# A depthwise convolution's sample rows as one GpSimd product and one VectorE sum, and four shifts of each tile moved from TensorE to VectorE

## The chip, the cores and the metric

The kernel runs on one core of one Trainium2 chip. The metric is the time of one execution on the device, in microseconds. A core has five engines that run side by side and wait for one another by semaphores: TensorE (PE in the profile; PEld is its loading of weights), VectorE (DVE), ScalarE (ACT), GpSimd (POOL) and SyncE (SP, which here issues DMAs). Each engine takes its own instructions strictly in the order in which the program issued them, so an instruction that waits holds up all that stand behind it on the same engine.

## The reference

The reference is one inference step of a small decoder trunk of two layers. It is run for a prompt of 256 tokens and for 8 samples of 4 new tokens each; both groups use the same weights. Layer 0 mixes tokens with sparse attention, layer 1 with a Conformer convolution module, and each mixer is followed by a feed-forward part that has a short convolution of its own. The change lies in the Conformer module of layer 1:

```python
def causal_dwconv(x_pad, w, b):
    c = x_pad.shape[-1]
    y = lax.conv_general_dilated(x_pad, w[:, None, :], window_strides=(1,), padding='VALID',
                                 dimension_numbers=('NWC', 'WIO', 'NWC'), feature_group_count=c)
    return y + b

def conformer_conv(x, hist, w_pw1, b_pw1, w_dw, b_dw, ln_g, ln_b, w_pw2, b_pw2):
    a, gate = jnp.split(x @ w_pw1 + b_pw1, 2, axis=-1)
    a = a * jax.nn.sigmoid(gate)
    a_pad = jnp.concatenate([hist, a], axis=1)
    h = jax.nn.silu(layer_norm(causal_dwconv(a_pad, w_dw, b_dw), ln_g, ln_b))
    return h @ w_pw2 + b_pw2, a_pad[:, -(CONV_WIDTH - 1):]
```

The width of the convolution is 31, there are 2048 channels, and every channel has its own 31 weights. For the prompt the 30 rows ahead of the first token are zero. For a sample they are rows of earlier tokens, given as an input; each of its 4 outputs is the sum of 30, 29, 28 or 27 products with given rows and 1, 2, 3 or 4 products with rows that this step computes.

## The kernel before

Activations lie with the channels on the 128 partitions: 16 tiles of 128 channels, each with 288 columns (256 of the prompt, then 8 times 4 of the samples). A matrix product with weights runs as float32 in three products of halves: ScalarE rounds a slab of weights to its high part (`pump`, L180), VectorE subtracts it from the slab for the low part (L182), and TensorE multiplies high by high, high by low and low by high (L259 to L261). The split slabs have three buffers, so the split of a slab runs at most a few slabs ahead of the matmuls that use it.

The order of all instructions is written out by the program, by a planner with lanes. `gemm` issues matmuls and after each piece calls `tick` with the microseconds that the piece is taken to last on PE. Each lane collects these as credit, and as long as it has credit it issues the next step of the generator at its head; a generator says with `yield` how much credit its step costs. Here the lanes are `ev` (what follows a group's matmuls), `bg` (`conv`) and `bg2` (`spread_out`), and `bg2` goes on only where `ev` is empty.

The Conformer module multiplies by `w_pw1` in 14 groups: two groups of two channel tiles each, then twelve groups of one. After a group, `glu` (L1746) writes the gated rows of tile j: those of the prompt into `apad` (L1760), those of the samples into the last four places of each of the 8 rows of `hist` (L1761). `past` holds the samples' sums over the given rows with the bias added; it was computed much earlier (`history`, L1677), by GpSimd products over shifted views (L1699) and VectorE sums (L1681).

The 31 taps of a prompt tile are shared out over three engines:

- ScalarE multiplies by the first `NACT` = 4 taps (L1808, L1811), and GpSimd adds these up (L1812) in the tile `ac`.
- VectorE adds the taps from `NACT` to `4 * PEM - 2`, one instruction of 256 columns each (L1824). With `PEM` = 3 these are the taps 4 to 10, seven of them. The first reads `ac`, the others go on in place in `cy`.
- TensorE takes the last 20 taps in 5 sets of 4 (L1840), each matmul with a 32-column block of a matrix `dg`, whose diagonals GpSimd fills with weights (L1801). Its moving operand `xt` holds shifted copies of the tile. SP writes the tile to DRAM (L1797) and reads it back in four pieces (L1819).

`spread_out(j)` (L1789) issues for a tile, in this order: the copy of its last rows (L1795), the write to DRAM, the `dg` product, the four ScalarE products with their adds, the four sample instructions (`samples`, L1780), the loads of `xt`, and the seven VectorE taps. `conv(j)` (L1828) then takes the mean from the tile on GpSimd (L1836, from tile 4 on), issues the matmuls, adds their result on VectorE (L1844), and lets `shifted` (L326) take the tile into the layer norm's sums (ScalarE square L330, GpSimd sums L335 and L336). Thus on GpSimd the instruction L1836 of one tile, which waits for the tile's last tap, stands ahead of the adds L1812 of the next.

`samples(j, d)` is one VectorE instruction: to the outputs from place d on it adds the new rows times the weight 30 - d. Four of them, for d = 0 to 3, with 32, 24, 16 and 8 elements for each partition, complete the samples' columns of a tile; the first also adds `past`.

Tile 15 has no group behind it that would hide it, and `conv_last` (L1857) computes it after the last group: its shifted copies come from matmuls (L1869) and ScalarE copies (L1871), and VectorE adds the taps 1 to 10 (L1885, L1887) with the sample instructions between them. L1891 joins both, and the layer norm follows. At the start of the stage `ready()` (L1739) issues two memsets and three DMAs on GpSimd, which at that time also adds to the sums of the layer norm before (L335, L336). These are then joined by VectorE (L356, L357) and summed over the partitions by PE (L372, L373).

Of the kernel before, what the change touches and what calls it, by code (L numbers as in the profile page):

```python
# [7 lines left out]
F32 = mybir.dt.float32  # L8
# [6 lines left out]
AF = mybir.ActivationFunctionType  # L15
OP = mybir.AluOpType
AX = mybir.AxisListType

D = 2048
NT = 16  # L20
TP = 256
NS, TS = 8, 4
# [8 lines left out]
CW = 31  # L31
# [16 lines left out]
NDG = 1  # L48
# [3 lines left out]
PRW = (6.0, 14.0, 9.0)  # L52
DOT = 0.35
DOTW = 5.0
PEM, NACT = 3, 4
BIS = (1.8, 0.3)
LST = (2.2, 2.2, 2.2, 1.5, 1.2, 0.9, 5.0)
ROPE = 0.5
# [6 lines left out]
ALAG = 5  # L65
LEADS = 12
SUBP = (1, 3)
CLAG = (3.2, 5.6, 5.0, 1.0)
LW = (1.2, 0.5, 0.8, 2.0, 1.4, 0.8, 16, 1.2, 1.45, 1.2)

QC, KC, VC, QIC, KIC = 0, 2048, 2560, 3072, 4096
# [574 lines left out]
def trunk(ctx, tc, a, o, stages=9):  # L646
    k = K(ctx, tc, a, o)
    nc = k.nc
# [19 lines left out]
    ap = st.enter_context(tc.tile_pool(name="attn", bufs=1))  # L668
# [42 lines left out]
    p = pb()  # L711
# [203 lines left out]
    def sample_index():  # L915
# [150 lines left out]
        for b in range(9):  # L1066
            s_ = 1 << b
            n_ = 512 - s_
            nc.vector.tensor_scalar(m[:, s_:], x_[:, s_:], 1 << (15 + b), None, op0=OP.bitwise_and)
            nc.vector.copy_predicated(x_[:, :n_], m[:, s_:], x_[:, s_:])  # L1070
            k.v(1.2)
            if p is None and (b == 8 or k.now > ready):
                p = total(1)
                nc.tensor.matmul(p[:, 1:2], lower, cnt, start=True, stop=True)
            yield LST[3]
# [598 lines left out]
    hist = hp.tile([128, NT, NS, CW - 1 + TS], F32, name="hist")  # L1674
    past = hp.tile([128, NT, NS * TS], F32, name="past")
# [32 lines left out]
    fp = sf.enter_context(tc.tile_pool(name="ffn0", reuse_waits="tile", bufs=1))  # L1708
# [15 lines left out]
    fp = sf.enter_context(tc.tile_pool(name="conf", reuse_waits="tile", bufs=1))  # L1724
    cy = fp.tile([128, NT, T], F32, name="cy")
# [8 lines left out]
    zero = fp.tile([128, last, CW], F32, name="zero")  # L1734
    tapm = fp.tile([128, 32], F32, name="tapm")
    wdq = fp.tile([128, NT * 32], F32, name="wdq")
    pads = {}

    def ready():  # L1739
        nc.gpsimd.memset(zero, 0.0)  # L1740
        nc.gpsimd.memset(lpad[:, 0:30], 0.0)
        nc.gpsimd.dma_start(tapm, a["consts"][:, CO["tapm"][0]:CO["tapm"][0] + 32])
        nc.gpsimd.dma_start(wdq, a["w_dq"])
        nc.gpsimd.dma_start(spread.rearrange("(j p) u -> p j u", p=128)[:, :, :CW], zero)
# [32 lines left out]
    dlane = Lane()  # L1777
    k.lanes.append(dlane)

    def samples(j, d):  # L1780

        sv = cy[:, j, TP:].rearrange("p (s t) -> p s t", t=TS)[:, :, d:]
        prev = past[:, j].rearrange("p (s t) -> p s t", t=TS) if d == 0 else sv
        nc.vector.scalar_tensor_tensor(sv, hist[:, j, :, CW - 1:CW - 1 + TS - d], k.par("w_dw", j * CW + CW - 1 - d),  # L1784
                                       prev, op0=OP.mult, op1=OP.add)

    spreads = {}

    def spread_out(j):  # L1789

        if j == 0:
            yield 10.0
        pad = pads.pop(j)
        t = pad[:, 30:]
        nc.gpsimd.tensor_copy(tailp[:, j], t[:, TP - CW + 1:])  # L1795
        rows = spread[j * 128:(j + 1) * 128]
        nc.sync.dma_start(rows[:, CW:], t)  # L1797
        nm = 8 - PEM
        dg = fp.tile([128, 4, nm, 32], F32, name="dg", bufs=2)
        wq = wdq[:, 32 * j:32 * j + 32].rearrange("p (i m) -> p i m", m=8)[:, :, PEM:]  # L1800
        nc.gpsimd.tensor_tensor(dg, wq[:, :, :, None].to_broadcast([128, 4, nm, 32]),  # L1801
                                tapm[:, None, None, :].to_broadcast([128, 4, nm, 32]), op=OP.mult)
        tap = lambda q_: (k.par("w_dw", j * CW + q_), pad[:, q_:q_ + TP])
        pl = fp.tile([128, TP], F32, name="ac", bufs=2)
        for q_ in range(NACT):
            w, src = tap(q_)
            if q_ == 0:
                nc.scalar.activation(pl, src, AF.Identity, bias=k.par("b_dw", j), scale=w)  # L1808
            else:
                d_ = fp.tile([128, TP], F32, name="ad", bufs=3)  # L1810
                nc.scalar.activation(d_, src, AF.Copy, scale=w)  # L1811
                nc.gpsimd.tensor_tensor(pl, pl, d_, op=OP.add)  # L1812
            yield CLAG[0] / 8
        for d in range(TS):
            samples(j, d)
            yield CLAG[0] / 8
        xt = fp.tile([128, 4, 284 - 4 * PEM], F32, name="xt", bufs=3)
        for i in range(4):
            nc.sync.dma_start(xt[32 * i:32 * i + 32],  # L1819
                              rows[:, i + 4 * PEM:i + 284].rearrange("(g c) u -> c g u", c=32))  # L1820
        acc = cy[:, j, :TP]
        for q_ in range(NACT, 4 * PEM - 1):
            w, src = tap(q_)
            nc.vector.scalar_tensor_tensor(acc, src, w, pl if q_ == NACT else acc, op0=OP.mult, op1=OP.add)  # L1824
            yield CLAG[1] / 7
        spreads[j] = dg, xt

    def conv(j):  # L1828
# [9 lines left out]
        for m in range(PEM, 8):  # L1838
            for i in range(4):
                nc.tensor.matmul(p[32 * i:32 * i + 32, :TP], dg[:, i, m - PEM],  # L1840
                                 xt[:, i, 4 * (m - PEM):4 * (m - PEM) + TP],
                                 start=m == PEM, stop=m == 7, skip_group_check=True)
        yield CLAG[2]
        nc.vector.tensor_tensor(cy[:, j, :TP], cy[:, j, :TP], p[:, :TP], op=OP.add)  # L1844
        if j < lnc.H:
            yield CLAG[3]
            lnc.first(j)
# [4 lines left out]
        else:  # L1852
            yield CLAG[3]
            lnc.shifted(j)
            yield 0.4

    def conv_last():  # L1857

        j = last
        k.drain(dlane)  # L1860
        lnc.stats(1)
        pc = pp()
        nc.tensor.matmul(pc[:, :T], nident, lnc.c, start=True, stop=False)
        w0 = 4 * LM - 1
        xt = fp.tile([128, 4, TP + 4 * (7 - LM)], F32, name="lxt")
        for g_ in range(4):
            ps_ = pp()
            for i in range(4):
                nc.tensor.matmul(ps_[32 * i:32 * i + 32, :xt.shape[2]], k.ident[:, 32 * g_:32 * g_ + 32],  # L1869
                                 lpad[:, w0 + i:w0 + i + xt.shape[2]], start=True, stop=True, skip_group_check=True)  # L1870
            nc.scalar.activation(xt[:, g_], ps_[:, :xt.shape[2]], AF.Copy)  # L1871
        lnc.stats()
        for q_ in range(1, NDG):
            nc.tensor.matmul(pc[:, :TP], diag[:, q_], lpad[:, q_:q_ + TP], start=False, stop=False)
        for m in range(LM, 8):
            for i in range(4):
                nc.tensor.matmul(pc[32 * i:32 * i + 32, :TP], ldg[:, i, m - LM],
                                 xt[:, i, 4 * (m - LM):4 * (m - LM) + TP],
                                 start=False, stop=False, skip_group_check=True)
        nc.tensor.matmul(pc[:, :TP], diag[:, 0], lpad[:, :TP], start=False, stop=True)  # L1880
        acc = cy[:, j, :TP]
        for q_ in range(NDG, w0):
            w, src = k.par("w_dw", j * CW + q_), lpad[:, q_:q_ + TP]
            if q_ == NDG:
                nc.vector.tensor_scalar(acc, src, w, k.par("b_dw", j), op0=OP.mult, op1=OP.add)  # L1885
            else:
                nc.vector.scalar_tensor_tensor(acc, src, w, acc, op0=OP.mult, op1=OP.add)  # L1887
            if q_ - NDG < TS:
                samples(j, q_ - NDG)
        nc.gpsimd.tensor_copy(tailp[:, j], lpad[:, 256:])  # L1890
        nc.vector.tensor_tensor(cy[:, j], cy[:, j], pc[:, :T], op=OP.add)  # L1891
        lnc.table()
        lnc.lag = 0
        lnc.shifted(j)
        k.pump(g_pw1[-1].first + len(g_pw1[-1].slabs) - 1)

    k.bg.cap, k.bg2.after = CAP, k.ev
    ready()
    dlane.append(diags())
    tailp = fp.tile([128, NT, CW - 1], F32, name="tailp")  # L1900
    for gi, g in enumerate(g_pw1):
# [11 lines left out]
        if js[-1] < last:  # L1913
            for j in js:
                k.bg2.append(spread_out(j))
                k.bg.append(conv(j))
    k.drain(k.bg2, k.bg, k.ev)
    conv_last()
    k.bg.cap, k.bg2.after = 3.0, None
    nc.gpsimd.dma_start(o["conv_p"].rearrange("p (j w) -> p j w", j=NT), tailp)  # L1920
# [99 lines left out]
def build(a):  # L2020
    import concourse.bacc as bacc
    nc = bacc.Bacc("TRN2", target_bir_lowering=False, num_devices=1)
    ins = {n: nc.dram_tensor(n, v.shape, mybir.dt.from_np(v.dtype), kind="ExternalInput").ap() for n, v in a.items()}
    outs = {n: nc.dram_tensor("out_" + n, s, F32, kind="ExternalOutput").ap() for n, s in _OUT.items()}
    with tile.TileContext(nc) as tc:
        with ExitStack() as ctx:
            trunk(ctx, tc, ins, outs)
    return nc
# [25 lines left out]
```

## Time and profile before

| | us |
|---|---|
| timed runs: lowest, median, highest of 3 | 2581.97, 2583.43, 2583.6 |
| the profiled execution, whole | 2581.04 |
| its span, from the first to the last instruction | 2579.2 |
| PE convolution matmuls L1840, first to last start | 1411.8 to 1588.7 |

The profile is one execution, taken by the hardware profiler. Its page gives each engine's busy time over the span, the chain of work that ended last, and the costliest groups of instructions. An engine's busy share over the whole span is an average over stages, so for one stage it is read from a table by windows. Rows of instructions give the start in us from the start of the span, the duration in us, the engine, the line of the program, the operation, what it writes and reads, shapes and count; a bracket at the end gives the engine's idle time just before and what ended it. Several instructions of one kind in a row are merged into one row with their count. On PE the matmuls are pipelined: each shows some 0.3 us, and yet a new one starts every 0.13 us. The page has the engines' share in the chain that ended last:

```profile
PE 88%; DVE 7%; ACT 2%; issue 2%; POOL 1%; DMA 1%; SPq 0%; another core or an unknown queue 0%; ACTq 0%; DVEq 0%; POOLq 0%
```

### The profile page before, as it was taken

To read this page: it belongs to the slowest core of one execution; us is meant where nothing else is said; L and a number is where in the kernel's file an instruction comes from. 1 tells how busy PE (TensorE), PEld (TensorE's weight loads), DVE (VectorE), ACT (ScalarE), POOL (GpSimd) and SP (SyncE) were. 2 spreads that over 40 slices of the span, in tenths; PEclk is the share of its full clock that TensorE was granted. 3 is DMA by queue.
4 is the path that set the end of the run, shared out by engine and by line. 5 is a ranking of instruction groups with operands and counts; after the bars stand their busy time and mean duration, and the time that the engine had idled before them with its cause. 6 is when DMAs were issued, how large, how long until landed. Compare 5 with 4: busy or idle time off the path is not lost.

```text
span 2579.2 us, 48375 instructions
## 1 busy us (share of the span) xinstructions
PE 2529.2 (98%) x19597; PEld 2434.7 (94%) x19597; DVE 1612.4 (63%) x2505; ACT 1172.3 (45%) x1864; POOL 653.6 (25%) x913
## 2 busy tenths in 40 slices
PE   9999899999999999999999999999999999999997
PEld 9789559999999999999999887999999999999997
DVE  5678446686665455555659997778555444555554
ACT  4464344564443334444446444656444333444444
POOL 1153541432221101011236564352010000111123
PEclk9999999999999999999999999999999999999999
DMA  9745865555555555556555655555545555555653
GB/s 349 211 129 193 284 230 185 165 177 188 161 169 167 159 172 162 167 163 162 177 164 171 181 165 182 163 165 164 166 162 172 164 160 168 163 170 163 172 164 103
DMA packets 152512, 454.81 MB, mean 176 GB/s; under 512 B 26224, under 2 KB 46880, under 8 KB 151008
## 3 DMA queue, kind: packets, MB, share of 16 engines
q1 hardware_dynamic: 139744, 400.04, 49.7%
q0 software_dynamic: 12016, 51.09, 5.8%
q8 instruction: 153, 2.51, 0.4%
q14 instruction: 71, 0.58, 0.1%
q10 hardware_dynamic: 528, 0.59, 0.1%
HBM read 438.37 MB, written 13.30 MB: 175 GB/s over the span
## 4 chain that ended last, share of the span: by engine, by line
PE 88%; DVE 7%; ACT 2%; issue 2%; POOL 1%; DMA 1%; SPq 0%; another core or an unknown queue 0%; ACTq 0%; DVEq 0%; POOLq 0%
PE pt L261 25%; PE pt L260 25%; PE pt L259 25%; DVE wl L182 2%; PE pg L259 2%; PE pg L261 2%; PE pg L260 2%; PE tr L1360 1%; DVE cy L1824 1%; PE pt L1840 1%; ACT wh L180 1%; PE m L1422 1%; PE pg L939 1%; PE sc L1381 0%; DVE cy L1784 0%
## 5 line engine op out<-in xcount | busy, mean ns | idle before, releaser
L182 DVE TENSOR_TENSOR wl<-raw,wh 128x1024 fp32r<-128x1024 f32 (+2 forms) x713 | 883.7, 1242 | 749.3 <-ACT wh L180 743.8
L180 ACT ACTIVATE wh<-raw 128x1024 fp32r<-128x1024 f32 (+1 forms) x732 | 761.8, 1044 | 836.4 <-PE pt L260 695.0
L261 PE MATMUL pt<-xh,wl 128*128 128x288 f32 (+1 forms) x3520 | 1040.1, 295 | 3.9 <-DVE wl L182 3.8
L260 PE MATMUL pt<-xl,wh 128*128 128x288 f32 (+1 forms) x3520 | 1041.9, 296 | 0.1
L259 PE MATMUL pt<-xh,wh 128*128 128x288 f32 (+1 forms) x3520 | 1041.0, 296 | 0.9 <-ACT xh L1481 0.9
L261 PEld LDWEIGHTS pt<-xh,wl 128*128 128x128 f32 x3520 | 665.4, 189 | 6.1 <-DVE wl L182 5.9
L259 PEld LDWEIGHTS pt<-xh,wh 128*128 128x128 f32 x3520 | 662.8, 188 | 7.7 <-issue 5.8
L260 PEld LDWEIGHTS pt<-xl,wh 128*128 128x128 f32 x3520 | 663.3, 188 | 0.4 <-DVE xl L1482 0.3
L261 PE MATMUL pt<-hh,wl 128*128 128x288 f32 (+1 forms) x1664 | 495.1, 298 | 0.0
L260 PE MATMUL pt<-hl,wh 128*128 128x288 f32 (+1 forms) x1664 | 493.8, 297 | 0.0
L259 PE MATMUL pt<-hh,wh 128*128 128x288 f32 (+1 forms) x1664 | 492.3, 296 | 0.0
L1597 POOL COPY sto<-gpad 128x2 f32<-128x2 f32 x88 | 85.2, 968 | 970.7 <-ACT gpad L1590 970.5
L260 PEld LDWEIGHTS pt<-hl,wh 128*128 128x128 f32 x1664 | 313.8, 189 | 0.1
L259 PEld LDWEIGHTS pt<-hh,wh 128*128 128x128 f32 x1664 | 313.4, 188 | 0.1
L261 PEld LDWEIGHTS pt<-hh,wl 128*128 128x128 f32 x1664 | 312.7, 188 | 0.0
L259 PE MATMUL pg<-xh,wh 128*128 128x288 f32 (+1 forms) x528 | 164.5, 312 | 0.8 <-ACT wh L180 0.8
L261 PE MATMUL pg<-xh,wl 128*128 128x288 f32 (+1 forms) x528 | 156.9, 297 | 1.8 <-DVE wl L182 1.7
L260 PE MATMUL pg<-xl,wh 128*128 128x288 f32 (+1 forms) x528 | 156.7, 297 | 0.6 <-DVE xl L285 0.4
L1601 ACT ACTIVATE s<-y,pvec 128x304 f32<-128x304 f32 x88 | 48.5, 551 | 161.2 <-DVE y L1596 161.2
L259 PEld LDWEIGHTS pg<-xh,wh 128*128 128x128 f32 (+1 forms) x528 | 99.3, 188 | 9.8 <-issue 7.9
L260 PEld LDWEIGHTS pg<-xl,wh 128*128 128x128 f32 (+1 forms) x528 | 99.2, 188 | 4.1 <-issue 2.6
L261 PEld LDWEIGHTS pg<-xh,wl 128*128 128x128 f32 (+1 forms) x528 | 99.3, 188 | 3.3 <-DVE wl L182 3.2
(370 smaller groups left out, 2289.9 us busy)
## 6 DMA issues: line engine op xcount, KB each, us to landing
raw<-w SPq DMA_DIRECT2D x705, 512.0 KB, 3.5
xt<-spread SPq DMA_DIRECT2D x60, 136.0 KB, 4.3
raw<-w SPq DMA_DIRECT2D x16, 296.0 KB, 6.6
kid<-kvt POOLq DMA_DIRECT2D x4, 1024.0 KB
kvt<-kid SPq DMA_DIRECT2D x8, 512.0 KB, 9.2
x<-xT POOLq DMA_DIRECT2D x1, 2304.0 KB
raw<-w SPq DMA_DIRECT2D x6, 384.0 KB, 3.1
out_y<-x SPq DMA_DIRECT2D x16, 144.0 KB, 1.8
```

Source lines behind the costliest of these rows:

```text
L180: nc.scalar.activation(wh[:, :n], r[:, :n], AF.Copy)
L182: eng.tensor_tensor(wl[:, :n], r[:, :n], wh[:, :n].bitcast(F32), op=OP.subtract)
L259: nc.tensor.matmul(out, wh[:, c:c + w], xh, start=st, stop=False)
L260: nc.tensor.matmul(out, wh[:, c:c + w], xl, start=False, stop=False)
L261: nc.tensor.matmul(out, wl[:, c:c + w], xh, start=False, stop=sp)
L939: nc.tensor.matmul(p[:, :512], qb[:, pr], kx[pr][:, 512 * i:512 * i + 512], start=True, stop=True)
L1360: nc.tensor.transpose(p[:, h * 128:(h + 1) * 128], g[:, h * 128:(h + 1) * 128], ident)
L1422: nc.tensor.matmul(po[32 * h:32 * h + 16, :128], z[:, c, i, h], g[:, 512 + h * 128:640 + h * 128], start=False, stop=(i == TS - 1 and c == ...
L1597: nc.gpsimd.tensor_copy(sto[:, j, 0:2], gp[:, 256:258])
L1601: nc.scalar.activation(s[:, :304], y[:, :304], AF.Silu, bias=k.par(bc, j))
L1824: nc.vector.scalar_tensor_tensor(acc, src, w, pl if q_ == NACT else acc, op0=OP.mult, op1=OP.add)
L1840: nc.tensor.matmul(p[32 * i:32 * i + 32, :TP], dg[:, i, m - PEM], xt[:, i, 4 * (m - PEM):4 * (m - PEM) + TP], start=m == PEM, stop=m == 7, ...
```

## The change

The samples' new rows are no longer four VectorE instructions. At the start of the stage GpSimd builds `wnew`, which has for each channel and each of the 4 output places a row of 4 weights, zero where a new row is later than the output. For each tile, ScalarE copies `past` into the fifth place of a tile `pn` of 8 samples by 4 outputs by 5; GpSimd multiplies a shifted view of the 4 new rows by the weights into the other four places (128 elements for each partition); three taps later VectorE sums the five. `PEM` goes from 3 to 4, so that TensorE takes 16 taps of tiles 0 to 14 in 4 sets, and VectorE eleven (4 to 14). `dg` and `xt` become smaller with it. The credits are changed: a tap costs 0.65 where it cost 0.8, and the samples one step of 0.4 where they had four. Tile 15 keeps its share of taps, with its samples done in the new way.

```diff
-PEM, NACT = 3, 4
+PEM, NACT = 4, 4
-CLAG = (3.2, 5.6, 5.0, 1.0)
+CLAG = (3.2, 0.65, 5.0, 1.0)
...
-    pads = {}
+    pads, pn = {}, {}
+    wnew = fp.tile([128, NT, TS, TS], F32, name="wnew")
 
     def ready():
+        news()
         nc.gpsimd.memset(zero, 0.0)
...
-    def samples(j, d):
-
-        sv = cy[:, j, TP:].rearrange("p (s t) -> p s t", t=TS)[:, :, d:]
-        prev = past[:, j].rearrange("p (s t) -> p s t", t=TS) if d == 0 else sv
-        nc.vector.scalar_tensor_tensor(sv, hist[:, j, :, CW - 1:CW - 1 + TS - d], k.par("w_dw", j * CW + CW - 1 - d),
-                                       prev, op0=OP.mult, op1=OP.add)
+    def news():
+
+        nc.gpsimd.memset(wnew, 0.0)
+        w = k.par("w_dw", 0, NT * CW).rearrange("p (j w) -> p j w", w=CW)
+        for t in range(TS):
+            nc.gpsimd.tensor_copy(wnew[:, :, t, TS - 1 - t:], w[:, :, CW - 1 - t:])
+
+    def samples(j, part):
+
+        if part == 0:
+            b_, w_ = hist[:, j], wnew[:, j]
+            win = bass.AP(tensor=b_.tensor, offset=b_.offset + CW - TS,
+                          ap=[list(b_.ap[0]), [CW - 1 + TS, NS], [1, TS], [1, TS]])
+            pn[j] = fp.tile([128, NS, TS, TS + 1], F32, name="pn", bufs=2)
+            nc.scalar.activation(pn[j][:, :, :, TS], past[:, j].rearrange("p (s t) -> p s t", t=TS), AF.Copy)
+            nc.gpsimd.tensor_tensor(pn[j][:, :, :, :TS], win, w_[:, None].to_broadcast([128, NS, TS, TS]), op=OP.mult)
+        else:
+            nc.vector.tensor_reduce(cy[:, j, TP:].rearrange("p (s t) -> p s t", t=TS), pn.pop(j), axis=AX.X, op=OP.add)
...
-        for d in range(TS):
-            samples(j, d)
-            yield CLAG[0] / 8
+        samples(j, 0)
+        yield CLAG[0] / 8
...
         for q_ in range(NACT, 4 * PEM - 1):
             w, src = tap(q_)
             nc.vector.scalar_tensor_tensor(acc, src, w, pl if q_ == NACT else acc, op0=OP.mult, op1=OP.add)
-            yield CLAG[1] / 7
+            if q_ == NACT + 2:
+                samples(j, 1)
+            yield CLAG[1]
...
-            if q_ - NDG < TS:
-                samples(j, q_ - NDG)
+            if q_ - NDG in (0, 3):
+                samples(j, (q_ - NDG) // 3)
```

## The prediction

> **What bounds the kernel now.** I read the page first, for the engine that sets the whole span, and then only the stretch that the change touches.
>
> ```profile
> PE 2529.2 (98%) x19597; PEld 2434.7 (94%) x19597; DVE 1612.4 (63%) x2505; ACT 1172.3 (45%) x1864; POOL 653.6 (25%) x913
> ```
>
> Over the span PE is the bound and DVE has a third of its time free. That average says nothing of the convolution, which lies between about 1380 and 1600 us. Busy time by window:
>
> ```profile
> core 0: us, PE busy (x) PEld busy (x) DVE busy (x) ACT busy (x) POOL busy (x), PEclk, DMA share, GB/s
> ...
> 1480.00:1500.00 20.00, 19.67 (x175) 17.75 (x168) 19.57 (x27) 9.83 (x16) 15.49 (x17) 1.00 0.59 159
> ...
> 1560.00:1580.00 20.00, 20.00 (x173) 18.74 (x173) 16.39 (x24) 9.85 (x17) 9.19 (x14) 1.00 0.43 147
> 1380.00:1590.00 210.00, 206.52 (x1855) 186.07 (x1854) 195.91 (x294) 100.10 (x172) 110.01 (x128) 1.00 0.62 182
> ```
>
> Here DVE is busy 195.91 of 210 us and in the middle 19.57 of 20: beside PE (206.52) there is a second full engine. Only from 1560 on does it have room. Who waits for whom in 1380 to 1590 (engine and line waited for, us, times, longest):
>
> ```profile
> POOL cy L1836 <- DVE cy L1824: 24.0, 9, 5.7
> ...
> PEld pt L261 <- DVE wl L182: 4.9, 6, 2.3
> ...
> DVE cy L1824 <- POOL ac L1812: 3.7, 3, 2.3
> ```
>
> PE already loses 4.9 us to weight splits (L182) that DVE brings late. The change gives DVE more to do in just this stretch, so the question is whether its added work exceeds its free 14.1 us.
>
> **The change part by part.**
>
> *Four matmuls fewer in each of 15 tiles (PEM 3 to 4).*
>
> ```profile
> 1411.76 2.37 PE L1840 MATMUL pt<-xt,dg 128*32 128x256 f32 x40
> ...
> 1411.76 1.89 PEld L1840 LDWEIGHTS pt<-xt,dg 128*32 128x32 f32 x40 [0.17 <-issue]
> ```
>
> The block is 40 records, two for each of 20 matmuls, loaded within 1.89 us; the loads are 0.11 long, so they start (1.89 - 0.11) / 39 = 0.046 us apart. Eight records go: 0.36 us a tile, 5.5 us in 15 tiles. The steps into and out of the block stay. This is the whole gain on PE, and it counts only where PE is what is late.
>
> *Four more shifts on DVE, four small samples instructions off it.* One cycle of a tile, DVE and then POOL:
>
> ```profile
> 1485.41 0.24 DVE L1761 SCALAR_TENSOR_TENSOR hist<-pt,pvec,sg 128x32 f32<-128x32 f32 x1
> 1485.57 0.24 DVE L1784 SCALAR_TENSOR_TENSOR cy<-hist,pvec,past 128x32 f32<-128x32 f32 x1
> 1485.85 2.28 DVE L1784 SCALAR_TENSOR_TENSOR cy<-hist,pvec,cy 128x24 f32<-128x24 f32 x3
> 1488.05 1.21 DVE L182 TENSOR_TENSOR wl<-raw,wh 128x1024 fp32r<-128x1024 f32 x1
> 1489.18 0.47 DVE L1824 SCALAR_TENSOR_TENSOR cy<-apad,pvec,ac 128x256 f32<-128x256 f32 x1
> 1489.69 0.48 DVE L1824 SCALAR_TENSOR_TENSOR cy<-apad,pvec,cy 128x256 f32<-128x256 f32 x1
> ```
>
> ```profile
> 1484.05 1.72 POOL L1836 TENSOR_TENSOR cy<-cy,lnc 128x288 f32<-128x288 f32 x1 [0.82 <-DVE cy L1824]
> 1485.73 2.37 POOL L1812 TENSOR_TENSOR ac<-ac,ad 128x256 f32<-128x256 f32 x3
> ```
>
> A shift that continues the one before starts 0.51 us after it (1489.18 to 1489.69), so four more are 2.04 us a tile; 0.40 us each, 1.6, where another instruction lies between. What the samples give back is the disputed term:
>
> ```profile
> L1784 DVE SCALAR_TENSOR_TENSOR cy<-hist,pvec,cy x48: 233/768/1268, 1392.2 to 1593.9; 128x24 f32<-128x24 f32 x16, 128x16 f32<-128x16 f32 x16, 128x8 f32<-128x8 f32 x16
> L1784 DVE SCALAR_TENSOR_TENSOR cy<-hist,pvec,past x16: 238/725/1352, 1391.5 to 1592.3; 128x32 f32<-128x32 f32 x16
> ```
>
> Least, median and longest ns: 0.24 us alone, some 0.75 us as a rule. By medians four are 3.0 us. But the cycle shows where that comes from: the last three of a tile (2.28 us) run beside the three POOL adds (2.37 us), one against one, and L1836 takes 1.72 us here. The two engines take turns. And the first shift (L1824, reads ac) needs the last of these adds, which come after L1836, which waited for the previous tile's last shift. If the small instructions go, DVE comes sooner to a shift that still has to wait for the same POOL chain. So they return between nothing and 3.0 us; I take their undisturbed spacing, 0.16 us (1485.41 to 1485.57), four times: 0.64 us.
>
> *The product on POOL and the sum on DVE.* Neither shape is in the trace. Nearest rows (least, median and longest ns):
>
> ```profile
> L1699 POOL TENSOR_TENSOR pr<-hist,pvec x32: 1165/1190/2018, 600.0 to 905.6; 128x496 f32<-128x496 f32 x32
> L1812 POOL TENSOR_TENSOR ac<-ac,ad x45: 729/737/1966, 1390.2 to 1581.2; 128x256 f32<-128x256 f32 x45
> L1795 POOL COPY tailp<-apad x15: 203/209/1203, 1384.3 to 1578.2; 128x30 f32<-128x30 f32 x15
> L1681 DVE TENSOR_REDUCE past<-pr x32: 659/662/665, 621.9 to 919.6; 128x16 f32<-128x496 f32 x32
> ```
>
> The product has 128 elements: (1.165 - 0.729) / 240 is 1.8 ns an element, so 0.73 - 0.23 = 0.50 us; ends 0.2 (the 30-element copy) and 0.73. It stands in POOL's queue right behind the third add, hence just ahead of the first shift, and DVE takes its turn after it: I charge 0.50. The dg product shrinks by 128 elements, 0.23 back. The sum reads 160 elements: between 0.24 (a small instruction) and 0.66 (496 elements) in proportion 0.35 us. It comes three shifts after the product, so it should not wait; if it did, the shifts and the next L182 behind it on DVE would, and PE for that. The copy of the past sums (32 elements) is on ACT, 100 of 210 us busy, which hides it; uncovered, 0.3 us a tile. Eleven shifts at 0.65 credits, with one yield for the samples, make 9.15 credits a tile for 8.8: issued 4% further apart, about what PE saves, so PE's pace stays. SP issues the same four loads of xt, 4 elements a row shorter.
>
> Per tile on DVE: 2.04 + 0.35 + 0.50 - 0.23 - 0.64 = **2.0 us**, ends 1.3 (shifts at 0.40, product at 0.2) and 2.7 (samples return nothing).
>
> *Start and end of the stage.* The new weights (a memset, four strided copies) stand first in POOL's queue at the layer's start.
>
> ```profile
> 1339.96 0.49 POOL L1740 MEMSET zero<- 128x465 f32 x1 [10.51 <-PE pt L261]
> ...
> 1345.28 1.52 DVE L357 TENSOR_TENSOR lns<-lns,lnsq 128x288 f32<-128x288 f32 x1
> ...
> 1345.41 0.75 PE L372 MATMUL pt<-lns,ones_d 128*128 128x288 f32 x2 [0.70 <-DVE lns L356]
> ```
>
> By the zero memset some 0.3 us, and 0.2 each for copies, as L1795's: 1.1 us that move POOL's DMA issues and its sums L335 and L336, for which L356 and L357 and then PE wait. Some slack lies between: 0 to 1.2, I take 0.4. In the last tile the sum stands before six shifts, and behind ACT's four L1871 copies, since the copy of the past sums comes after them in ACT's queue.
>
> ```profile
> 1593.92 1.78 ACT L1871 ACTIVATE lxt<-pt 128x272 f32<-128x272 f32 x4 [2.55 <-PE pt L1869]
> ...
> 1594.08 3.09 DVE L1887 SCALAR_TENSOR_TENSOR cy<-lpad,pvec,cy 128x256 f32<-128x256 f32 x6
> ...
> 1599.36 0.45 DVE L1891 TENSOR_TENSOR cy<-cy,pt 128x288 f32<-128x288 f32 x1 [2.20 <-PE pt L1880]
> ```
>
> ACT is free at 1595.7, the copy done at 1596.0, the sum at 1596.4, six shifts (3.09) at 1599.5: the 2.20 us of cover is just used up. 0 to 0.8, I take 0.4.
>
> **Sum.** DVE's 195.9 + 15 x 2.0 = 225.9; the 3.7 us for the adds stay idle: 229.6 for 210, **+19.6 us**. PE's saving lies under that; only the last three tiles, where DVE had room, keep 3 x 0.36 = 1.1. With 0.8 for the two ends: +19.3 on the profiled execution's 2581.04 (span 2579.2), 2600.3. The three timed runs (2581.97 to 2583.6, median 2583.43) lie up to 2.6 above it: I forecast **2601**. Its own range, with 1.3 and 2.7 a tile: 2590 to 2613.
>
> **Rivals.**
>
> *The waits leave with the small instructions.* If DVE finds splits (L182) to do while POOL adds, four instructions take their whole 3.0 us along and DVE stays even (2.0 + 0.64 - 3.0 = -0.4 a tile). Then PE's 5.5 us count, less 0.8: -4.7, 2577 to 2579. If DVE's relief also ends the late splits (4.9 us in the waits), -9, about 2573. For it: the removed kind has the most stretched rows. Against it: L182 reads two tensors as the shifts do and would take turns with the adds itself, and the first shift waited for the adds even with the samples as cover (3.7 us).
> The Trainium skill, "GPSIMD Engine Reference", section "1. Specifications", says that GpSimd shares its SBUF interfaces with VectorE and contends with DVE instructions in a 2-port mode or with two SBUF inputs. By that rule four contending instructions make way for one that does not (the sum has one input), which is this rival; the trace agrees that such instructions are stretched, but the four added shifts are of the same kind.
>
> *The loop closes.* Last shift, L1836, three adds, product, first shift of the next tile run strictly one after the other, with the splits outside: over 2.7 us a tile, +32 to +40, 2613 to 2621. For it: POOL waited 24.0 us in L1836 for DVE. Against it: the first four tiles have no L1836, the last three have room.
>
> **Chances.** Forecast 0.57; closed loop 0.09; waits leave 0.34, of it 0.14 with no more than the 4.7 us and 0.20 with late splits ended too. A measurement of this kernel tells about 0.2% (5 us) from no change: faster 0.20, same 0.14, slower 0.66. For 8 in 10 the range goes from 2576 (into the even case) to 2613; some 0.12 lies below and 0.08 above.
>
> **What would show it.** Right: DVE over 95% busy in every window of the stage to 1590 and later, the stage 15 to 20 us longer, PE's waits for L182 grown from 4.9 to some 20 us, and L1824 waiting for POOL more than 3.7 us. Wrong: L1824's mean near 0.48 with L182 near 1.2 us, PE waiting no more than before, or the sum waiting for the product. If the first shifts start right after the adds without DVE idle, the samples' term was mis-sized.

## The result, and the profile after

The changed kernel takes 2600.16 us (median of six runs, 2597.37 to 2604.11) against 2582.7 for the kernel before (six runs): a ratio of 1.0067, 95% interval 1.0056 to 1.0078. The profiled execution took 2597.37 us, its span is 2595.6 us, 16.4 more than before. In the changed kernel the VectorE taps are line L1837 (before L1824), GpSimd's adds L1826 (L1812), the mean L1851 (L1836), TensorE's convolution matmuls L1855 (L1840) and the VectorE addition of their result L1859 (L1844).

All of the difference arises in the convolution stage. The first weights of the product that follows it (L238) are loaded here, in the kernel before and then in the changed one (start, duration, and in the bracket the idle time just before with its releaser):

```profile
1605.82 0.29 PEld L238 LDWEIGHTS pt<-xh,wh 128*128 128x128 f32 x1 [5.17 <-ACT xh L426]
```

```profile
1622.19 0.29 PEld L238 LDWEIGHTS pt<-xh,wh 128*128 128x128 f32 x1 [5.17 <-ACT xh L426]
```

That is 16.37 us later; what follows takes 973.4 us in both (2579.2 - 1605.82 and 2595.6 - 1622.19). The first tap of each tile, grouped over all tiles (least, median and longest ns, then first and last start), shows the loss as a slower rhythm. Before, and after:

```profile
L1824 DVE SCALAR_TENSOR_TENSOR cy<-apad,pvec,ac x15: 469/478/1015, 1396.4 to 1582.0; 128x256 f32<-128x256 f32 x15
```

```profile
L1837 DVE SCALAR_TENSOR_TENSOR cy<-apad,pvec,ac x15: 471/650/659, 1392.6 to 1598.2; 128x256 f32<-128x256 f32 x15
```

Over 14 steps that is (1582.0 - 1396.4) / 14 = 13.26 us a tile before and (1598.2 - 1392.6) / 14 = 14.69 after: 1.43 more, and the last first tap starts 16.2 us later. The first one starts 3.8 us earlier, since no sample instructions stand ahead of it any more.

So far this looks like the forecast. But VectorE did not become busier. The page's line of engines after:

```profile
PE 2531.2 (98%) x19477; PEld 2436.5 (94%) x19477; DVE 1610.2 (62%) x2517; ACT 1173.9 (45%) x1880; POOL 657.5 (25%) x934
```

DVE's busy time fell from 1612.4 to 1610.2 us with 60 taps more. A window in its middle and the whole (columns as in the prediction: for each engine busy us and instructions, then PE's granted clock, DMA share, GB/s):

```profile
1480.00:1500.00 20.00, 17.01 (x143) 15.44 (x142) 14.27 (x25) 6.80 (x11) 11.25 (x15) 1.00 0.60 167
...
1380.00:1590.00 210.00, 193.88 (x1603) 173.72 (x1602) 180.68 (x287) 95.02 (x175) 106.70 (x133) 0.96 0.56 165
```

From 1480 to 1500 DVE is busy 14.27 us where it had been 19.57, and PE 17.01 where it had been 19.67: neither of the two engines that were full before is full any more. Two engines wait for each other in a circle. The waits of the changed kernel from 1380 to 1605 (engine and line waited for, us, times, longest):

```profile
POOL lns L335 <- DVE cy L1859: 40.5, 9, 6.1
...
DVE cy L1837 <- POOL ac L1826: 27.3, 12, 4.1
PEld pt L261 <- DVE wl L182: 18.4, 12, 2.4
...
POOL cy L1851 <- DVE cy L1837: 11.0, 6, 3.4
```

DVE's wait for the adds grew from 3.7 to 27.3 us, and PE's wait for the weight splits (L182) from 4.9 to 18.4. One cycle shows how. First DVE, then GpSimd, in order of time:

```profile
1492.24 1.22 DVE L182 TENSOR_TENSOR wl<-raw,wh 128x1024 fp32r<-128x1024 f32 x1
1496.48 0.65 DVE L1837 SCALAR_TENSOR_TENSOR cy<-apad,pvec,ac 128x256 f32<-128x256 f32 x1 [3.02 <-POOL ac L1826]
```

```profile
1486.73 0.98 POOL L335 TENSOR_TENSOR lns<-lns,cy 128x288 f32<-128x288 f32 x1 [3.95 <-DVE cy L1859]
1487.67 0.99 POOL L336 TENSOR_TENSOR lns<-lns,lnsq 128x288 f32<-128x288 f32 x1
1488.61 0.41 POOL L1809 COPY tailp<-apad 128x30 f32<-128x30 f32 x1
1488.97 2.03 POOL L1815 TENSOR_TENSOR dg<-wdq,tapm 128x512 f32<-128x512 f32 x1
1492.40 1.72 POOL L1851 TENSOR_TENSOR cy<-cy,lnc 128x288 f32<-128x288 f32 x1 [1.41 <-DVE cy L1837]
1494.08 2.36 POOL L1826 TENSOR_TENSOR ac<-ac,ad 128x256 f32<-128x256 f32 x3
1496.40 0.44 POOL L1797 TENSOR_TENSOR pn<-hist,wnew 128x128 f32<-128x128 f32 x1
```

GpSimd stands 3.95 us until DVE has joined the tile before (L1859), works through L335, L336, the copy and the `dg` product, stands 1.41 us more until DVE has done the last tap, and only then comes to the mean and the three adds. The first tap needs the last of these adds. DVE, which the removed sample instructions would have kept busy just here, stands 3.02 us at the head of its queue with that first tap. The splits that PE will need stand behind it.

### The profile page after: what moved, and what is told of

It reads as the page before. It is cut to its first block, busy times and chain, and to the rows that moved or that the text cites. A ratio compares the mean times of both kernels' runs of the same rounds, so it can differ in the third digit from the quotient of the medians.

```text
span 2595.6 us, 48200 instructions
## 1 busy us (share of the span) xinstructions
PE 2531.2 (98%) x19477; PEld 2436.5 (94%) x19477; DVE 1610.2 (62%) x2517; ACT 1173.9 (45%) x1880; POOL 657.5 (25%) x934
## 4 chain that ended last, share of the span: by engine, by line
PE 77%; DVE 4%; POOL 2%; issue 1%; ACT 1%; DMA 0%; SPq 0%; ACTq 0%; DVEq 0%; POOLq 0%
PE pt L261 25%; PE pt L260 25%; PE pt L259 25%; DVE wl L182 2%; DVE cy L1837 1%; POOL ac L1826 1%; PE pt L1855 0%; ACT wh L180 0%; POOL x L419 0%; PE m L1422 0%; POOL cy L1851 0%; PE pt L372 0%; PE tr L1360 0%; DMA xt<-spread 0%; DVE apad L1762 0%
## 5 line engine op out<-in xcount | busy, mean ns | idle before, releaser
L182 DVE TENSOR_TENSOR wl<-raw,wh 128x1024 fp32r<-128x1024 f32 (+2 forms) x713 | 882.5, 1240 | 748.7 <-ACT wh L180 745.0
L259 PE MATMUL pt<-xh,wh 128*128 128x288 f32 (+1 forms) x3520 | 1043.5, 296 | 1.1 <-ACT xh L1481 0.9
L259 PEld LDWEIGHTS pt<-xh,wh 128*128 128x128 f32 x3520 | 665.0, 189 | 8.0 <-issue 4.9
L259 PE MATMUL pt<-hh,wh 128*128 128x288 f32 (+1 forms) x1664 | 492.4, 296 | 0.0
L259 PEld LDWEIGHTS pt<-hh,wh 128*128 128x128 f32 x1664 | 313.5, 188 | 0.1
L259 PE MATMUL pg<-xh,wh 128*128 128x288 f32 (+1 forms) x528 | 164.6, 312 | 1.4 <-ACT wh L180 0.8
L259 PEld LDWEIGHTS pg<-xh,wh 128*128 128x128 f32 (+1 forms) x528 | 99.6, 189 | 10.4 <-issue 7.9
```

The costliest lines, as they stand in the source:

```text
L182: eng.tensor_tensor(wl[:, :n], r[:, :n], wh[:, :n].bitcast(F32), op=OP.subtract)
L259: nc.tensor.matmul(out, wh[:, c:c + w], xh, start=st, stop=False)
```

## The experiments

The forecast's time held while its account of DVE's time did not. The runs are there to settle three things: whether the samples' edit gives anything, whether the loss comes from DVE's work or from the wait, and what the taken-away matmuls are worth. All medians are in us; the kernel before is the one that ran on the same chip.

| run | median | before | ratio (95%) |
|---|---|---|---|
| e1_samples_only | 2585.11 | 2582.99 | 1.0008 (0.9999 to 1.0018) |
| e2_taps_only | 2601.07 | 2582.99 | 1.0069 (1.0052 to 1.0086) |
| e3_adds_first | 2601.03 | 2582.99 | 1.0066 (1.0050 to 1.0083) |
| e4_adds_first_old | 2583.61 | 2582.99 | 1.0002 (0.9992 to 1.0011) |
| e5_prep_ahead | 2590.56 | 2583.49 | 1.0025 (1.0016 to 1.0035) |
| e6_prep_ahead_old | 2583.98 | 2583.49 | 1.0000 (0.9990 to 1.0010) |
| e7_seven_shifts | 2578.07 | 2583.49 | 0.9978 (0.9968 to 0.9988) |
| e8_prep_ahead_three | 2580.75 | 2583.22 | 0.9994 (0.9984 to 1.0004) |
| e9_prep_ahead_even | 2585.24 | 2583.22 | 1.0009 (0.9999 to 1.0019) |
| e10_after_even | 2599.72 | 2583.22 | 1.0063 (1.0045 to 1.0081) |
| e11_mixed | 2582.72 | 2584.47 | 0.9993 (0.9984 to 1.0002) |

### The samples' edit alone, the taps alone

The changed kernel with the taps shared out as before (`CLAG[1]` keeps a tile's credits at 8.8):

```diff
-PEM, NACT = 4, 4
+PEM, NACT = 3, 4
-CLAG = (3.2, 0.65, 5.0, 1.0)
+CLAG = (3.2, 0.97, 5.0, 1.0)
```

> Only the samples are done in the new way; PEM stays 3 (seven shifts on VectorE), and a shift costs 0.97 credits, so that a tile keeps its 8.8. Theory (the first shift of a tile waits for GpSimd's chain of L1836, three adds and now the product; the four old sample instructions had only filled that wait): time 2580 to 2587, VectorE idle before the first shift grown from 3.7 to 15 us or more although its busy time in the stage falls by some 30 us. Rival (the samples' instructions cost VectorE their whole 3 us a tile): VectorE has room, PE's waits for L182 fall from 4.9 to under 2 us, and the time falls by 3 to 5 us, 2578 to 2580.

Measured: no difference (table). Waits from 1380 to 1605, then the window of the stage:

```profile
DVE cy L1837 <- POOL ac L1826: 43.2, 14, 5.3
...
PEld pt L261 <- DVE wl L182: 8.6, 10, 2.3
```

```profile
1380.00:1590.00 210.00, 203.78 (x1809) 183.43 (x1811) 160.09 (x247) 101.39 (x185) 116.56 (x142) 1.00 0.57 176
```

DVE's busy time falls from 195.91 to 160.09, by 35.8 us, its wait for the adds rises from 3.7 to 43.2, by 39.5, and the time stays. The small instructions had filled a wait and nothing else: taking them out turns busy time into idle time, about one for one.

The kernel before with four more taps a tile on DVE, its sample instructions as they were:

```diff
-PEM, NACT = 3, 4
+PEM, NACT = 4, 4
-CLAG = (3.2, 5.6, 5.0, 1.0)
+CLAG = (3.2, 5.95, 5.0, 1.0)
...
-            yield CLAG[1] / 7
+            yield CLAG[1] / 11
```

> Only the shifts are moved: PEM 4 (eleven shifts on VectorE, four sets on TensorE), with the four old sample instructions; a shift costs 0.54 credits, a tile 9.15 as in the changed kernel. Theory (four more shifts of 0.5 us lengthen the chain from one tile's first shift to the next one's, and the old sample instructions hide behind the adds): 2594 to 2604, about the changed kernel's 2600, with VectorE idle for the adds little and PE's waits for L182 at 12 to 20 us. Rival (the new samples, with product and wait, make the loss): 2578 to 2586.

Measured: 1.0069, the whole loss of the full change. Waits from 1380 to 1605, then the window of the stage:

```profile
PEld pt L261 <- DVE wl L182: 21.2, 17, 2.6
...
DVE cy L1824 <- POOL ac L1812: 2.3, 2, 1.5
```

```profile
1380.00:1590.00 210.00, 189.64 (x1579) 170.76 (x1578) 201.49 (x326) 93.72 (x162) 103.06 (x123) 0.98 0.55 158
```

Here DVE is as full as the forecast had it (201.49 us of 210; 19.43 of 20 in the window from 1500), hardly waits for the adds (2.3 us), and PE waits for splits. The changed kernel has the same ratio within the intervals with 180.68 us busy and 27.3 us of that wait. Both halves together say: the loss is that of the taps, and the samples' edit gives nothing back of it.

A full DVE is no proof here that its work sets the pace. One cycle of e2_taps_only, GpSimd and then DVE:

```profile
1498.09 1.72 POOL L1836 TENSOR_TENSOR cy<-cy,lnc 128x288 f32<-128x288 f32 x1 [1.41 <-DVE cy L1824]
1499.77 1.55 POOL L1812 TENSOR_TENSOR ac<-ac,ad 128x256 f32<-128x256 f32 x2
```

```profile
1499.89 1.73 DVE L1784 SCALAR_TENSOR_TENSOR cy<-hist,pvec,cy 128x24 f32<-128x24 f32 x3
1501.54 0.48 DVE L1824 SCALAR_TENSOR_TENSOR cy<-apad,pvec,ac 128x256 f32<-128x256 f32 x1
```

The mean again waits 1.41 us for the last tap, the adds again come behind it, and the sample instructions run beside these adds until the first tap can start. So the same circle can be in this kernel, with the wait filled. The rhythm of its first taps is nearly the same too: 14.59 us a tile (1398.2 to 1602.4) and 14.69 in the changed kernel.

### The adds issued ahead

If the wait for the adds is what costs, the adds of tile j + 1 should be issued ahead of the mean of tile j, which holds them up. In the changed kernel, and in a second run in the kernel before:

```diff
         yield CLAG[0] / 8
+        added.add(j)
         xt = fp.tile([128, 4, 284 - 4 * PEM], F32, name="xt", bufs=3)
...
         dg, xt = spreads.pop(j)
+        while j + 1 < last and j + 1 not in added:
+            yield 0.3
```

> The changed kernel, but each tile's L1836, matmuls and what follows are issued only after the adds and the product of the next tile have been issued, so that on GpSimd the next tile's adds stand ahead of the instruction that waits for this tile's last shift. Theory (the loop last shift, L1836, adds, product, first shift sets the pace): the 27 us that VectorE is idle before first shifts fall under 8, PE's waits for L182 under 8, and the time to 2580 to 2588. Rival (VectorE's own work, with four more shifts, is what is too long): idle time turns into busy time or moves to other places, and the time stays at 2595 to 2602.

> The same reordering on the kernel before. Theory: the adds are ready before the first shift, the sample instructions no longer run beside them and fall from a median of 0.75 us towards 0.25; VectorE's few idle waits for adds (3.7 us) go and PE's 4.9 us of late splits shrink: 2577 to 2582. Rival (before, the loop did not bind): within 2 us of 2582.7.

Measured: 1.0066, no gain; its theory missed. The waits of e3_adds_first (its taps are L1838, the joining of a tile L1862):

```profile
POOL lns L335 <- DVE cy L1862: 46.3, 8, 6.7
DVE cy L1838 <- POOL ac L1826: 28.2, 11, 3.5
```

The adds now stand ahead of the mean, but still behind L335 of the tile before, and that waits for DVE's joining: the same circle over another instruction, 28.2 us instead of 27.3. The order of two neighbours in GpSimd's queue was the wrong handle; what must change is how far ahead of the taps the whole preparation is issued. On the kernel before (1.0002) the move does nothing.

### The whole preparation one tile ahead

Copy, write to DRAM, `dg`, ScalarE products, adds, the samples' product and the loads of `xt` become a generator of their own, stepped after each tap of the tile before, so that GpSimd has no tap to wait for between them. `dg` also gets a third buffer; in the changed kernel its product (L1815) had waited for a free one only once, for 1.2 us. The core of it:

```diff
+        preps[j] = pad, dg, pl, xt
+
+    ahead = {}
+
+    def spread_out(j):
...
+        if j not in preps:
+            yield from ahead.pop(j, None) or prep(j)
...
-            yield CLAG[1]
+            if q_ > NACT and j + 1 in pads and j + 1 not in preps:
+                if j + 1 not in ahead:
+                    ahead[j + 1] = prep(j + 1)
+                next(ahead[j + 1], None)
+            yield 0.83
```

> The changed kernel, but what a tile needs ahead of its first shift (tail copy, dg, ScalarE products, GpSimd adds, samples' product, loads of xt) is issued during the shifts of the tile before, so on GpSimd it stands ahead of L335 and L336 of the tile before that as well; dg gets a third buffer, a shift costs 0.83 credits. Putting only L1836 behind the adds had left VectorE idle for 28 us, with GpSimd waiting in L335 for VectorE's L1844. Theory (the adds come late because they stand behind some GpSimd instruction that waits for VectorE): idle before first shifts under 6 us, PE's waits for L182 under 8, and 2575 to 2585. Rival (VectorE with eleven shifts is full, and the idle time was only where its waits happen to show): no idle time, but VectorE busy over 19.4 of 20 in the middle of the stage and 2594 to 2602.

> The same issue one tile ahead on the kernel before (seven shifts, four old sample instructions; a shift 1.03 credits, a tile 8.8 as before). Theory: there the waits were small (3.7 us of idle time, 4.9 us of late splits), so at most these go: 2577 to 2583. Rival (the order does not matter with seven shifts): within 2 us of 2583.

Measured: 1.0025 with eleven taps, 1.0000 on the kernel before with seven taps and its old sample instructions. Waits from 1380 to 1605 in e5_prep_ahead (taps L1846, adds L1823), then one of its windows:

```profile
PEld pt L261 <- DVE wl L182: 15.4, 14, 2.6
...
DVE cy L1846 <- POOL ac L1823: 8.7, 4, 3.9
```

```profile
1480.00:1500.00 20.00, 17.61 (x138) 16.01 (x136) 19.68 (x27) 5.25 (x9) 13.77 (x17) 0.91 0.47 125
```

The wait for the adds falls to 8.7 us, DVE is full again (19.68 of 20 where it had been 14.27), and the loss over the kernel before goes from 17.5 us to 7.1. So about 10 us of the loss went with the circle; some 7 remain, with DVE full at this pace of issue, and PE still waits 15.4 us for splits. The theory of 2575 to 2585 was missed. On the kernel before, where the wait was short (3.7 us), the order is worth nothing.

Two settings of the same kernel. With seven taps again, the tap's credit is 1.26 (its total as before):

```diff
-PEM, NACT = 4, 4
+PEM, NACT = 3, 4
...
-            yield 0.83
+            yield 1.26
```

> New samples and the issue one tile ahead, but PEM 3: seven shifts on VectorE, five sets on TensorE (a shift 1.26 credits). Issuing ahead took VectorE's idle time away and left it busy 19.7 of 20 with eleven shifts. Theory (four shifts a tile are what fills VectorE): with seven, idle and busy both shrink, VectorE is under 18 of 20 busy, PE's waits for L182 are under 6 us and the time is 2579 to 2584, as before or a little better. Rival (the new samples load VectorE or GpSimd as much as the old): PE's waits stay at 8 us or more and the time over 2585.

And with eleven taps further apart, so that they don't crowd the splits:

```diff
-            yield 0.83
+            yield 0.92
```

> Issue one tile ahead with eleven shifts as in the earlier run, but a shift costs 0.92 credits, so that the tiles follow one another more slowly and the backlog of the first four tiles is worked off later. Theory (VectorE is full on average over the whole stage): 2587 to 2593, as with 0.83. Rival (it is full only while the backlog is worked off, and has room after it): PE's waits fall by half and the time to 2580 to 2586.

Measured: 0.9994 and 1.0009, both with an interval that takes in 1. The waits of e8_prep_ahead_three:

```profile
DVE wl L182 <- ACT wh L180: 13.3, 13, 2.5
...
PEld pt L261 <- DVE wl L182: 2.3, 1, 2.3
```

DVE now waits for ScalarE's rounding, which follows PE, and PE waits for splits 2.3 us in all: DVE is no longer what holds PE up, and PE, which has all 20 matmuls of a block again, is busy 207.90 of 210 us. The wait of e9_prep_ahead_even:

```profile
PEld pt L261 <- DVE wl L182: 7.3, 9, 2.1
```

Spacing the taps halves PE's wait (15.4 to 7.3 us), and the kernel is level with the one before. Yet in the profiled execution its L238 starts at 1611.69, 5.9 us after that of the kernel before. Taps put off may be taps left over when the last group ends; that is not shown. The same spacing in the changed kernel itself:

```diff
-CLAG = (3.2, 0.65, 5.0, 1.0)
+CLAG = (3.2, 0.75, 5.0, 1.0)
```

> The changed kernel with a shift at 0.75 credits for 0.65, a tile at 10.25 for 9.15. Theory (each tile's chain from first shift over L1836 and the adds to the next first shift is some 14 us, longer than the 12.2 us at which tiles are issued): at some 13.5 us a tile PE's waits shrink, 2586 to 2595. Rival (the pace of issue does not matter, the work of VectorE does): 2597 to 2603.

Measured: 1.0063, no gain that the intervals tell from 1.0067; the theory was missed. PE's wait for splits went from 18.4 to 14.8 us, L238 started at 1628.9 instead of 1622.2. Spacing alone does not open the circle.

### The matmuls' share alone

The changed kernel without the taps 7 to 10 of the tiles 0 to 14; they are left out of the convolution, while the shorter PE block and the samples' edit stay.

```diff
             w, src = tap(q_)
+            if 7 <= q_ < 11:
+                yield CLAG[1]
+                continue
```

> The changed kernel without four of its eleven shifts (taps 7 to 10 of tiles 0 to 14 are left out, their credits are kept). This has the shorter matmul block without the work that it put on VectorE. Theory: 15 times four shifts of 0.5 us are gone, the waits of PE fall to those of the kernel before, and the 5.5 us of the matmuls show: 2575 to 2581. Rival (the new samples and the order of issue cost by themselves): 2583 to 2592.

Measured: 0.9978, or 5.4 us faster than the kernel before. The block and the next weight matmul, before (whose block, starting at 1411.76, the prediction quotes) and in this kernel:

```profile
1414.06 0.40 PE L259 MATMUL pt<-xh,wh 128*128 128x288 f32 x1
```

```profile
1411.32 1.93 PE L1858 MATMUL pt<-xt,dg 128*32 128x256 f32 x32
1413.18 0.40 PE L259 MATMUL pt<-xh,wh 128*128 128x288 f32 x1
```

From the block's start to the next L259 it takes 2.30 us before and 1.86 here: 0.44 us a tile, 6.6 in 15. Of that 5.4 show in the time. Hence the four taps cost the changed kernel 22 us (2600.16 - 2578.07; by the ratios, 1.0067 - 0.9978 = 0.0089 of 2583, 23), 1.5 us a tile, against 2.0 us of DVE time at their undisturbed spacing.

The wait alone is no loss. In this kernel DVE waits even longer for the adds than in the changed one:

```profile
DVE cy L1840 <- POOL ac L1826: 28.8, 12, 4.1
```

In e1_samples_only it waits 43.2 us, and neither of the two is told to be slower than the kernel before. The wait is in all three; what the changed kernel has besides is four more taps in each round.

### Is there a version that beats both?

What PE gains is to be had only where DVE has room, in the late tiles. This one prepares ahead, has seven taps up to tile 8 and eleven from tile 9 on (the edit against e8_prep_ahead_three):

```diff
+    pem = lambda j: PEM + (j >= 9)
...
-            yield 1.26
+            yield 8.8 / (4 * pem(j) - 1 - NACT)
```

> New samples, issue one tile ahead, seven shifts and five sets for tiles 0 to 8, eleven shifts and four sets (PEM 4) for tiles 9 to 14, where VectorE was under 18.3 of 20 busy with seven shifts throughout. Theory (a shift on VectorE costs nothing where VectorE has room, and then the shorter matmul block shows): 6 x 0.36 = 2.2 us under the run with seven shifts (2580.8), 2577 to 2580, below both kernels. Rival (the room is needed, late tiles delay the end of the stage as with even pace): 2582 to 2588.

Measured: 0.9993 (0.9984 to 1.0002), as good as e8_prep_ahead_three (0.9994) and no better. PE waits 8.2 us for splits where that one had 2.3, which is more than six shorter blocks save (2.6 us). So no version with the whole convolution was found that measures faster than the kernel before.

## Why the prediction came out

The forecast of 2601 us was met by the time, 2600.16. Its terms were not all met; some errors offset one another.

**The disputed term, what the samples return.** The prediction took 0.64 us a tile with bounds of 0 and 3.0, and argued that without the small instructions "DVE comes sooner to a shift that still has to wait for the same POOL chain". This is right, and the lower bound holds: e1_samples_only gains nothing. The choice inside the bounds was 0.64 a tile too high. In busy time the opposite end is nearer: the 64 sample instructions of the kernel before were busy for 43.6 us, 2.7 a tile. Against them stand the taps, which went from 62.5 to 99.1 us, and the sums with 5.0, and DVE's busy total fell by 2.2. None of it shortened anything.

**The sum.** The step "DVE's 195.9 + 15 x 2.0 = 225.9; the 3.7 us for the adds stay idle" does not describe the changed kernel. Busy time went down, and the idle time for the adds became 27.3. The sum treated DVE as full; in the changed kernel DVE is a link of a circle with GpSimd, and some 10 of the 17.5 us go away when the preparation is issued ahead (e5_prep_ahead). That the sum gave nearly the same number was partly luck. e2_taps_only, with DVE full and little wait for the adds, looks like the forecast's own mechanism, but its sample instructions may fill the same wait. Eleven taps with the old sample instructions and the preparation ahead were not run, so how much of the loss in e2_taps_only is DVE's own work stays open.

**The marks.** "DVE over 95% busy in every window" was wrong (14.27 of 20 us). "PE's waits for L182 grown from 4.9 to some 20" (18.4), "L1824 waiting for POOL more than 3.7 us" (27.3) and the stage longer by 15 to 20 us (16.4) were right. Of the rivals, "the waits leave with the small instructions" fell with e1_samples_only. "The loop closes" was right that the instructions come to run one after the other, and too high in its price: it set +32 to +40 us, and 16.4 were measured. It had put the splits outside the round, and the cycle above has one inside, at 1492.24 while DVE waits.

**PE's saving** was put at 0.36 us a tile and measured 0.44 (e7_seven_shifts). The prediction took the mean spacing of 40 loads, 0.046 us; the 32 loads of the shorter block take 1.45 us where 40 took 1.89, so the eight that left were 0.055 apart.

**Product, sum and copy.** Grouped over the tiles of the changed kernel:

```profile
L1796 ACT ACTIVATE pn<-past x16: 241/246/262, 1390.7 to 1612.0; 128x32 f32<-128x32 f32 x16
L1797 POOL TENSOR_TENSOR pn<-hist,wnew x16: 439/447/702, 1392.6 to 1609.4; 128x128 f32<-128x128 f32 x16
L1799 DVE TENSOR_REDUCE cy<-pn x16: 305/312/321, 1396.7 to 1612.3; 128x32 f32<-128x160 f32 x16
```

The product takes 0.45 us (0.50 forecast), the sum 0.31 (0.35), the copy 0.25 (0.3): the proportions between the nearest rows were good to a tenth or so. But the product does not delay the first tap by its length: at 1496.40 it starts behind the adds, and the tap at 1496.48 runs beside it, stretched from 0.47 to 0.65 us.

**The start** was put at 0.4 us and cost nothing measurable. GpSimd's queue at that point in the changed kernel:

```profile
1339.73 0.31 POOL L1784 MEMSET wnew<- 128x256 f32 x1 [10.38 <-PE pt L260]
1340.10 0.88 POOL L1787 COPY wnew<-pvec 128x16 f32<-128x16 f32 x4
```

These are the 1.1 us that were estimated, yet PE takes up its next group at 1346.8, no later than before (1347.2): the slack between GpSimd's sums and PE was enough.

**The tail** was put at 0.4 and came to 0.1. From the last group's last matmul to L238 it takes 15.3 us before (1590.5 to 1605.8) and 17.4 after (1604.8 to 1622.2). Most of that difference is tile 14's block, which stands among the last group's matmuls before (at 1586.67) and behind them after. PE's first sums of the layer norm (L372) behind the last group, before and then after:

```profile
1590.67 0.65 PE L372 MATMUL pt<-lns,ones_d 128*128 128x288 f32 x2
```

```profile
1605.07 1.93 PE L1855 MATMUL pt<-xt,dg 128*32 128x256 f32 x32
1606.93 0.75 PE L372 MATMUL pt<-lns,ones_d 128*128 128x288 f32 x2
```

From there to L238 it takes 15.15 us before and 15.26 after. The mean of tile 14 does run late, behind the last group, because its first tap waited 3.49 us for the adds:

```profile
1606.50 0.80 POOL L1851 TENSOR_TENSOR cy<-cy,lnc 128x288 f32<-128x288 f32 x1 [7.90 <-DVE cy L1837]
```

PE has its own work at that time, though. The cover that the prediction weighed for the sum before six shifts just held: the last of them ends at 1615.6, and TensorE's part of the last tile at 1615.7.

**What wasn't foreseen** is PE's clock (below). From 1380 to that first L372 (1590.67 before, 1606.93 after) PE's idle time went from 3.5 to 17.2 us, 13.7 more, and its busy time from 207.2 to 209.8, 2.6 more. The shorter blocks should have taken 6.6 us out of the busy time; the 9.2 us between are about what five stretches of 3.41 us at half rate cost (8.5). It is bookkeeping of one execution, not a price of each part. A PE that runs slower may also wait less for splits, and e2_taps_only loses as much with a clock of 0.98. Of the changed kernel's six timed executions, two had a mean clock of 0.994 and took 2600.12 and 2600.21 us; the profiled one had 0.991 and took 2597.37. So no run shows that the slow stretches lengthen the time.

## What to carry to other kernels

Small instructions that stand in front of a wait can be free, however long they last in the profile: before counting them as gain, ask what the instruction behind them waits for. When work is added to an engine that already trades results with a second one in every round, follow one round through both queues before adding up busy time, because the wait can take the place of the load and the sum will look right for the wrong reason. Here DVE's reserve of 14 us in 210 was no place for 30 us of work taken from PE: the move lost time until the tiles' preparation was issued a tile ahead, and then it only broke even.

## What the runs showed of the hardware

**TensorE fell to half rate after some gaps of about 2 us, and the traces show after which.** In the changed kernel, PE rows around a wait of 1.88 us for a split:

```profile
1386.49 0.41 PE L261 MATMUL pt<-xh,wl 128*128 128x290 f32 x1 [1.88 <-DVE wl L182]
...
1387.49 0.44 PE L261 MATMUL pt<-xh,wl 128*128 128x290 f32 x1
1387.73 0.45 PE L259 MATMUL pt<-xh,wh 128*128 128x290 f32 x1
```

Behind the gap the matmuls come to stand 0.24 us apart (1387.49 to 1387.73), where they stood 0.13 apart before it. The kernel before had a gap of 2.10 us on PE at the same place, up to 1387.12, and none of this.

The granted clock tells the two apart. In all thirteen profiles it changes only at the points of a grid with steps of 3.413 us. In the changed kernel five half-rate stretches, of one step each, start between 1380 and 1590, at 1387.27, 1472.61, 1499.91, 1537.46 and 1568.18; these are 25, 8, 11 and 9 steps apart. The two steps around the gap, in the changed kernel and then in the kernel before (columns as above):

```profile
1383.85:1387.27 3.42, 1.54 (x12) 1.31 (x10) 3.42 (x6) 3.42 (x8) 1.50 (x3) 1.00 0.19 65
1387.27:1390.68 3.41, 3.41 (x17) 3.41 (x16) 3.41 (x5) 3.41 (x8) 0.91 (x1) 0.50 0.75 173
```

```profile
1382.35:1385.76 3.41, 2.67 (x20) 2.44 (x19) 3.41 (x6) 3.41 (x7) 3.28 (x4) 1.00 0.70 190
1385.76:1389.18 3.42, 2.06 (x15) 2.06 (x16) 3.42 (x5) 3.42 (x9) 0.22 (x1) 1.00 0.26 73
```

In the changed kernel the gap falls into one step, PE is idle for 1.88 us of it, and the next step has half the clock. In the kernel before a point of the grid cuts the gap into 0.74 and 1.36 us of idle time, and the clock stays. Counting idle time by the matmuls' ends as the profile models them, over the thirteen profiles from 20 to 2570 us, every step at full clock in which PE was idle for 1.80 us or more (49 of them) was followed by a half-rate step. No step with less than 1.47 us was; of the 27 in between, 12 were. The Trainium skill, "TensorE: Matmul & The Clock Gate", section "Part 1: The HAM clock gate", says that TensorE goes to 4/8 of its clock after an idle window of about 3.4 us, and that this window runs freely. The trace agrees with the half rate (0.24 against 0.13 us) and with a window of that length that runs freely, but the window need not be idle throughout: 1.8 us of it were enough here.

**DVE and GpSimd stretch each other.** The mean takes 1.72 us beside a split (1492.40, quoted above) and 0.80 alone (1606.50); a tap takes 0.65 us beside the new product and 0.47 without.
